# A decoder trunk in float32: the last 512 channels of each sub-layer as one 512-wide piece in halves of K, instead of two pieces of 256

## The chip, the core and the metric

The kernel runs on one core of one Trainium2 chip. The metric is device time in microseconds (us) of one execution; several runs are made and the median is taken. A profiled execution, one more run, gives the trace that is read here. Its times are in us from the start of its span. Engines: PE is TensorE, PEld its weight loads, DVE is VectorE, ACT is ScalarE, POOL is GpSimd, SP is SyncE (its queue issues most DMAs).

## The reference

Two layers over 256 tokens of 2048 channels, in float32. Each layer has two sub-layers, and each sub-layer ends in the same way: a product with a weight matrix, an RMS norm over the 2048 channels of a token, a gain, and the addition to the residual x.

```python
for li in range(DEPTH):                                  # DEPTH = 2
    h = rmsnorm(x, g_mix_pre[li])
    proj = einsum('bsd,de->bse', h, w_in[li])            # 2048 -> 5120
    # four mixers of 512 channels each: gMLP, differential attention, dilated attention, convolution
    mixed = concatenate([out_a, out_b, out_c, out_d], axis=-1)
    x = x + rmsnorm(einsum('bse,ed->bsd', mixed, w_out[li]), g_mix_post[li])
    h = rmsnorm(x, g_ffn_pre[li])
    f = square(relu(einsum('bsd,df->bsf', h, w_ff1[li])))    # 2048 -> 8192
    x = x + rmsnorm(einsum('bsf,fd->bsd', f, w_ff2[li]), g_ffn_post[li])
```

with `rmsnorm(x, g) = x * rsqrt(mean(x*x) + 1e-6) * g`.

## The kernel before

**Numbers in two parts.** Every float32 matrix product is made of three: a value is split into a high part h (rounded to the fp32r type) and a low part l (the rest), and the kernel adds h·h, h·l and l·h. Weights arrive from HBM as "units" of 128 x 1024 floats (512 KB), in the order in which they are used. For each unit ACT makes h (1024 elements per partition) and DVE makes l. `split_hi` and `split_lo` (L251, L261) issue these; a split needs a free buffer pair, of which there are six, and two more from the ending of the mixing on (`room_for`, L269). A buffer is given back by `done(u)` (L289), so a split that reuses it waits for the last matmul of the unit `u`. An h split of ACT in the trace is `h<-w`, an l split of DVE `l<-w,h`.

**Two kinds of products.** In channel form (`unit_c`, `group_c`) the weights are the stationary operand and the tokens stream; the results, tiles `acc` and `accg`, feed the next step. In token form (`unit_t` L432, `units_t` L449, through `mm_t` L406) 128 tokens are stationary and the weights stream; the result has tokens on partitions. `unit_t` makes 512 channels for both halves of the tokens (t = 0, 1) at once: two PSUM tiles `acct`, a unit of 1024 weights covers two steps of K = 128, and for each step kk it calls `mm_t` for t = 0 and t = 1. One `mm_t` is three matmuls.

**A sub-layer's ending** (`sublayer_end`, L681) is what the change touches. There are four of them: mixing and FFN of two layers. Of the 2048 output channels the first three pieces of 512 are made by `unit_t`. The last 512 are made by two calls of `units_t` with n = 256. Each call has four units (a unit covers four steps of K) and makes all of K for the first 128 tokens, tile `accu`, then all of K for the other 128 tokens. So an ending has 4 x 48 = 192 matmuls of 256 columns, and token half 0 is complete 48 matmuls before token half 1. After each accumulation a follow-up is put into the list `soon` (`later`, L378):

- `y_block` (L662) adds the partial sum yt to PSUM (DVE, in FFN endings alone), then squares it with a sum over the channels (ACT, `junk<-accu` or `junk<-yt`, into `sy`), and multiplies by the gain (DVE, `yt<-...,gpb`). For the last piece, n == 4, it returns after the square, and the gain is done beside the Sqrt.
- `last_in` (L695) then, for n == 4, sets the flags calm, held and end, runs `y_rms` (L606: sum, Sqrt on ACT, gain on DVE, reciprocal and two small DVE steps) and puts `turn` into the list `front`, or `finish` in the last ending.
- `turn_part` (L629) handles a quarter of 512 channels of one token half: X is updated on DVE, PE transposes four blocks (`turned`), ACT writes the high part of the next layer's operand (`xhl<-turned,prm`, four steps), and DVE the low part. Then `have[t]` is raised.
- `group_c` (L466) follows at once: the next product. Its blocks are `(0,0), (1,0), (2,0), (0,1), ...` as (quarter, token half); a block (q, 0) has 16 matmuls of 256 columns and needs quarter q of token half 0. So token half 0 is turned while PE still works on token half 1.
- In the last ending `finish` (L654) updates X and writes the output instead.

`sqrt_soon` (L717) runs a tiny Sqrt on ACT between the two calls of `units_t`, so that its table is there.

**What sets the order.** The engines' queues are in program order, and a small planner at build time writes it. `Paced` (L75) keeps a planned clock for each engine, by the cost functions of L117 to L131: a matmul of N columns costs N/2400 + 0.003 us, a DVE step (70 + N)/960 or, for scalar_tensor_tensor, (128 + N)/960, an ACT step (140 + N)/1200. Before every `mm_t` the code calls `pump` (L368), which issues all follow-ups that are due by PE's planned clock. Only there does other work enter the queues. A follow-up is due D_ = 0.13 planned us after what it needs (0.2 for the first step of `later`), and an engine may be ahead of PE's clock by 1.5 planned us at most, 1.0 when the flag end is set. A step (`step`, L357) looks in this order: a split that is needed soon, `soon`, `front`, other splits. With held set, low splits stop. If `group_c` needs a quarter that is not yet issued, `force` (L372) lets time pass without matmuls.

**Buffers.** `pacc` holds four PSUM tiles of one bank; before, a 256-wide `accu` takes one of them.

Of the kernel before, what the change touches and what calls it, by code (L numbers as in the profile page):

```python
# [11 lines left out]
F32 = mybir.dt.float32  # L12
# [3 lines left out]
ALU = mybir.AluOpType  # L16
# [3 lines left out]
P = 128  # L20
L = 2
D = 2048
T = 256
GW = 512
FF = 8192
KD = D // P
# [3 lines left out]
HALF = 8  # L30
# [104 lines left out]
def trunk_kernel(ctx, tc, xT, xt, wu, par, gpost, gw, gb, lam, ndist, mult, out):  # L135
# [9 lines left out]
    tiny = ctx.enter_context(tc.tile_pool(name="tiny", bufs=2))  # L145
    pacc = ctx.enter_context(tc.tile_pool(name="pacc", bufs=4, space=PSUM))
# [8 lines left out]
    V, S = Paced(nc.vector, _dve_cost, PE), Paced(nc.scalar, _act_cost, PE)  # L155
# [121 lines left out]
    def use(u, low=True):  # L277

        state["cur"] = max(state["cur"], u)
        while state["hi"] <= u:  # L280
            split_hi()
        if not low:
            return
        while state["lo"] <= u:
            if state["hi"] <= state["lo"]:
                split_hi()
            split_lo()

    def done(u):  # L289
        wh.pop(u)  # L290
        wl.pop(u)
        pool_of.pop(u)
# [4 lines left out]
    unit = [0]  # L297
    soon, front, queue, lanes, back = [], [], [], [None, None], []
# [32 lines left out]
    def entry(g):  # L331
        return [g, None, lambda: True]
# [35 lines left out]
    def pump():  # L368
        while step():
            pass  # L370

    def force(cond):  # L372
        now = PE.t
        while not cond():
            if not step() and not step(now):
                now += 0.2

    def later(f, n=1):  # L378

        held[0] += n  # L380

        def g():
            yield S, t
            yield from f()
            held[0] -= n

        t = PE.t + 0.2
        soon.append(entry(g()))
# [17 lines left out]
    def mm_t(ps, u, w, xhl, kk, t):  # L406

        h = xhl[:, kk, t * P : (t + 1) * P]
        l = xhl[:, kk, T + t * P : T + (t + 1) * P]
        PE.matmul(ps, h, wh[u][:, w], start=kk == 0, stop=False)  # L410
        PE.matmul(ps, h, wl[u][:, w], start=False, stop=False)
        PE.matmul(ps, l, wh[u][:, w], start=False, stop=kk == KD - 1)
# [33 lines left out]
            done(u)  # L446
        return pss

    def units_t(xhl, n, after):  # L449

        c = HALF * P // n
        units = range(unit[0], unit[0] + KD // c)
        unit[0] += KD // c
        for t in range(2):
            force(lambda: held[0] < 4)
            ps = pacc.tile([P, n], F32, tag="acc", name=f"accu{units[0]}_{t}")
            for kk in range(KD):
                u, k = units[kk // c], kk % c
                use(u)
                pump()  # L460
                mm_t(ps, u, slice(k * n, (k + 1) * n), xhl, kk, t)
                if t == 1 and k == c - 1:
                    done(u)
            later(lambda ps=ps, t=t: after(ps, t))

    def group_c(rhs, have, order, us):  # L466

# [138 lines left out]
    def y_rms(t, sy, beside):  # L606

        yield V, S.t + D_
        ss, a, s, r0, r = [tiny.tile([P, 1], F32, tag=f"y{j}", name=f"y{j}") for j in range(5)]
        V.reduce_sum(ss, sy[:, t, :], axis=AX.X)  # L610
        S.activation(s, ss, AF.Sqrt, bias=epst, scale=1.0 / D)
        V.tensor_scalar(a, ss, -0.5 / D, -0.5 * EPS, ALU.mult, ALU.add)
        beside()
        V.reciprocal(r0, s)
        V.scalar_tensor_tensor(a, a, r0, r0, ALU.mult, ALU.mult)
        V.scalar_tensor_tensor(r, a, 1.5, r0, ALU.add, ALU.mult)
        return r

    def turn(t, r, sx, xhl, li, gcol, have):

        yield None, lambda: True
        if t == 0:
            state["turned"] = 0
        for q in range(4):
            n = TURNS.index((t, q))
            place = sum(e[3] < n for e in front if len(e) > 3)
            front.insert(place, entry(turn_part(t, q, n, r, sx, xhl, li, gcol, have)) + [n])
# [26 lines left out]
    def finish(t, r):  # L654

        yield V, 0.0
        for n in range(4):
            c = slice(GW * n, GW * (n + 1))
            V.scalar_tensor_tensor(X[:, t, c], yt[:, t, c], r, X[:, t, c], ALU.mult, ALU.add)
            Q.dma_start(out[:, t, c], X[:, t, c])  # L660

    def y_block(ps, t, c, n, add, sy):  # L662


        y = yt[:, t, c]
        if add:
            yield V, 0.0
            V.tensor_tensor(y, ps, y, ALU.add)
            ps = y
            yield S, V.t + D_  # L670
        if sy is not None:
            junk = ev.tile([P, GW], F32, tag="junk", name="junk", bufs=1)
            S.activation(junk[:, 0 : c.stop - c.start], ps, AF.Square, accum_out=sy[:, t, n : n + 1])
            if n == 4:
                return ps
            yield V, 0.0
            V.tensor_tensor(y, ps, gpb[:, c], ALU.mult)
        elif not add:
            S.activation(y, ps, AF.Copy)

    def sublayer_end(rhs, first, add, li, gcol, n0=0):  # L681

        nonlocal xhl
        sy = tiny.tile([P, 2, 5], F32, tag="sy", name="sy", bufs=1)
        sx = tiny.tile([P, 2, 4], F32, tag="sx", name="sx", bufs=1)
        have, us = [0, 0], []
        pss = first
        for n in range(3):
            if pss is None:
                pss = unit_t(rhs)  # L690
            for t in range(2):
                later(lambda ps=pss[t], t=t, n=n: y_block(ps, t, slice(GW * n, GW * (n + 1)), n, add, sy))
            pss = None

        def last_in(ps, t, n):  # L695
            c = slice(T * (n + 3), T * (n + 4))
            y = yield from y_block(ps, t, c, n, add, sy)
            if n == 4:
                state["calm"] = state["held"] = state["end"] = li is not None
                r = yield from y_rms(t, sy, lambda: V.tensor_tensor(yt[:, t, c], y, gpb[:, c], ALU.mult))  # L700
                g = finish(t, r) if li is None else turn(t, r, sx, xhl, li, gcol, have)
                front.insert(0, entry(g))

        if li is not None:
            xhl = big.tile([P, KD, 2 * T], F32R, tag="xhl", name="xhl")
        units_t(rhs, T, lambda ps, t: last_in(ps, t, 3))
        sqrt_soon()
        units_t(rhs, T, lambda ps, t: last_in(ps, t, 4))
        if li is None:
            force(idle)  # L710
            return None, None
        state["calm"] = True
        group_c(xhl, have, ((0, 0), (1, 0), (2, 0), (0, 1), (1, 1), (2, 1), (3, None)), us)
        state["calm"] = state["end"] = False
        return us, sx
# [410 lines left out]
def _pack_weights(w_in, w_out, w_ff1, w_ff2):  # L1126

    parts = []

    def blocked(w):  # L1130

        k, n = w.shape
        return w.reshape(k // 1024, 8, P, n // P, P).transpose(3, 0, 2, 1, 4).reshape(n // P, k // 1024, P, 1024)

    def tokens(w):

        n = w.shape[1]
        return w.reshape(-1, 1024 // n, P, n).transpose(0, 2, 1, 3).reshape(-1, P, 1024)

    def grouped(b):  # L1140

        b = b.reshape(2, 2, 2, P, 2, 4 * P)
        return b.transpose(2, 4, 0, 3, 1, 5).reshape(-1, P, 1024)

    def ending(w):
        return [tokens(w[:, n * GW : (n + 1) * GW]) for n in range(3)] + [tokens(w[:, n * T : (n + 1) * T]) for n in (6, 7)]

    for li in range(L):
        w = w_in[li]
        first = []  # L1150
        rest = []
        for kind, grp, i in IN_ORDER:
            if kind == "c":
                b = blocked(w[:, grp * GW + i * P : grp * GW + (i + 1) * P])[0]
            else:
                b = tokens(w[:, grp * GW : (grp + 1) * GW])
            (first if len(first) < 4 else rest).append(b)
        parts.append(grouped(np.stack(first)))
        parts += rest
        wo = np.concatenate([w_out[li][g * GW : (g + 1) * GW] for g in OUT_GROUPS])  # L1160
        parts += ending(wo)
        f1 = blocked(w_ff1[li])
        for blk in range(4):
            b = f1[blk * KD : (blk + 1) * KD]
            if blk == 0:
                parts.append(grouped(b[:4]))
                b = b[4:]
            parts.append(b.reshape(-1, P, 1024))
            b = w_ff2[li][blk * D : (blk + 1) * D]
            parts += ending(b) if blk == 3 else [tokens(b[:, n * GW : (n + 1) * GW]) for n in range(4)]  # L1170
    return np.ascontiguousarray(np.concatenate(parts))
# [48 lines left out]
```

## Time and profile before

| | us |
|---|---|
| median of 3 runs | 2134.38 (2134.36 to 2135.84) |
| profiled execution, its own time | 2133.36 |
| span of the profiled execution | 2131.6 |
| PE busy | 2115.2 |
| PEld busy | 1821.5 |
| DVE busy | 1417.9 |
| ACT busy | 1100.3 |
| mean granted clock of TensorE | 0.998 |

The time of an execution is the span and what lies around it, here 1.8 us. Busy times of engines overlap. An engine's row in the trace gives start and length in us, engine, operation, tile written and tiles read, the shape, and in brackets how long the engine was idle before it and what ended that idle time. Nearly all instructions are issued by a helper, so that their line is L99 everywhere; the tile names tell them apart. The four endings' `accu` pieces begin at 329.2, 1041.0, 1388.7 and 2100.4 us (mixing, FFN, mixing, FFN).

### The profile page before, as it was taken

The page shows a single profiled execution, that of the slowest core. Times are in us where ns is not written, and L with a number is a line of the kernel's source. Part 1 is how long each engine was busy: PE and PEld are TensorE (multiplying, and loading weights), DVE is VectorE, ACT ScalarE, POOL GpSimd, SP SyncE. Part 2 cuts the span into 40 slices and gives each one's busy share as a digit, 9 for nine tenths or more (in the row PEclk, how much of TensorE's full clock was granted, in tenths as well). Part 3 has the DMA queues.
Part 4 walks back from the last instruction along what each step waited for, and adds up shares of the span by engine and source line. Part 5 has one row for each costly group of instructions (what it writes and reads, how often), then busy time and mean ns, then how long its engine had stood idle before and what let it go on. Part 6 is the DMA issues. An engine that isn't in the chain of part 4 may idle for free.

```text
span 2131.6 us, 29947 instructions
## 1 busy us (share of the span) xinstructions
PE 2115.2 (99%) x11404; PEld 1821.5 (85%) x11404; DVE 1417.9 (67%) x2207; ACT 1100.3 (52%) x1711; POOL 9.9 (0%) x57
## 2 busy tenths in 40 slices
PE   9999999999999999999999999999999999999998
PEld 7888889888888888888888888898888888888887
DVE  6889666764665675576579886568547656755754
ACT  6556856554543453454465568565444434434542
POOL 0000000000000000000000000000000000000000
PEclk9999999999999999999999999999999999999999
DMA  7645474565555555555454455646655555555563
GB/s 242 221 147 186 158 237 159 198 226 190 187 197 190 189 192 193 191 192 190 167 171 148 167 170 179 224 159 194 220 196 184 193 197 187 190 197 189 188 197 109
DMA packets 110256, 400.20 MB, mean 188 GB/s; under 512 B 12512, under 2 KB 12800, under 8 KB 109344
## 3 DMA queue, kind: packets, MB, share of 16 engines
q1 hardware_dynamic: 109296, 393.93, 55.2%
q0 software_dynamic: 672, 4.36, 0.6%
q8 instruction: 89, 1.46, 0.3%
q14 instruction: 55, 0.45, 0.1%
q10 hardware_dynamic: 144, 0.01, 0.0%
HBM read 396.15 MB, written 2.10 MB: 187 GB/s over the span
## 4 chain that ended last, share of the span: by engine, by line
PE 96%; DVE 1%; ACT 1%; DMA 1%; issue 0%; DVEq 0%; ACTq 0%
PE acct L99 44%; PE acc L99 42%; PE accu L99 4%; PE accg L99 3%; PE sc L99 1%; DMA w<-in_wu 1%; PE od L99 0%; DVE X L99 0%; PE tr L99 0%; PE turned L99 0%; ACT h L99 0%; PE z L99 0%; DVE l L99 0%; ACT L99 0%; PE ob L99 0%
## 5 line engine op out<-in xcount | busy, mean ns | idle before, releaser
L99 DVE TENSOR_TENSOR l<-w,h 128x1024 fp32r<-128x1024 f32 (+1 forms) x738 | 896.2, 1220 | 543.1 <-ACT h L99 403.9
L99 ACT ACTIVATE h<-w 128x1024 fp32r<-128x1024 f32 (+1 forms) x738 | 775.8, 1055 | 555.0 <-PE acct L99 389.0
L99 PE MATMUL acc<-xhl,h 128*128 128x512 f32 x2560 | 615.6, 391 | 0.0
L99 PE MATMUL acct<-h,f 128*128 128x512 f32 x1920 | 592.4, 389 | 0.0
L99 PEld LDWEIGHTS acc<-xhl,h 128*128 128x128 f32 x2560 | 469.6, 188 | 91.7 <-issue 1.3
L99 PEld LDWEIGHTS acct<-h,f 128*128 128x128 f32 x1920 | 360.4, 188 | 74.7
L99 PE MATMUL acct<-l,f 128*128 128x512 f32 x960 | 373.5, 389 | 0.0
L99 PEld LDWEIGHTS acc<-xhl,l 128*128 128x128 f32 x2560 | 328.6, 191 | 13.2 <-issue 1.0
L99 PE MATMUL acc<-xhl,l 128*128 128x256 f32 x2560 | 335.3, 283 | 0.0
L99 PEld LDWEIGHTS acct<-l,f 128*128 128x128 f32 x960 | 180.2, 188 | 37.1
L99 PE MATMUL acct<-h,xhl 128*128 128x512 f32 x512 | 169.0, 398 | 0.0
L99 ACT ACTIVATE evr<-acc 128x256 f32<-128x256 f32 x160 | 61.4, 385 | 157.3 <-PE acc L99 157.2
L99 ACT ACTIVATE f<-u 128x256 fp32r<-128x256 f32 x120 | 50.1, 417 | 136.7 <-DVE u L99 136.6
L99 PE MATMUL acct<-h,mhl 128*128 128x512 f32 x384 | 120.2, 391 | 0.0
L99 PEld LDWEIGHTS acct<-h,xhl 128*128 128x128 f32 x512 | 96.2, 188 | 20.2 <-issue 0.7
L99 DVE SCALAR_TENSOR_TENSOR cacc<-ch,prm,cacc 128x256 f32<-128x256 f32 x240 | 102.5, 484 | 0.0
L99 PE MATMUL acct<-l,xhl 128*128 128x512 f32 x256 | 100.1, 391 | 1.0 <-DVE l L99 1.0
L99 PE MATMUL accg<-xhl,h 128*128 128x256 f32 (+1 forms) x400 | 89.4, 323 | 6.1 <-DVE xhl L99 6.1
L99 PEld LDWEIGHTS acct<-h,mhl 128*128 128x128 f32 x384 | 72.1, 188 | 14.9
L99 PEld LDWEIGHTS accg<-xhl,h 128*128 128x128 f32 x400 | 65.6, 192 | 11.3 <-DVE xhl L99 4.7
L99 PE MATMUL acct<-l,mhl 128*128 128x512 f32 x192 | 74.7, 389 | 0.0
L99 DVE TENSOR_TENSOR u<-acc,evr 128x256 f32<-128x256 f32 x120 | 50.9, 424 | 23.9 <-ACT evr L99 22.7
(182 smaller groups left out, 1356.1 us busy)
## 6 DMA issues: line engine op xcount, KB each, us to landing
w<-in_wu SPq DMA_DIRECT2D x734, 512.0 KB, 3.3
gpb<-in_gpost POOLq DMA_DIRECT2D x4, 1024.0 KB, 5.1
X<-in_xt SPq DMA_DIRECT2D x2, 1024.0 KB, 6.4
out<-X SPq DMA_DIRECT2D x8, 256.0 KB, 2.0
x_in<-in_xT SPq DMA_DIRECT2D x3, 512.0 KB, 6.5
w<-in_wu SPq DMA_DIRECT2D x4, 256.0 KB, 5.4
wT<-in_gw SPq DMA_DIRECT2D x2, 512.0 KB, 4.4
x_in<-in_xT SPq DMA_DIRECT2D x2, 256.0 KB, 4.6
```

The source lines that it names most:

```text
L99: return f(*a, **k)
```

## The change

A new loop, `units_end`, takes the place of the two calls of `units_t`. It makes the last 512 channels in one piece: two PSUM tiles of 128 x 512, eight units of two steps of K each. It runs the first half of K for token half 0, then for token half 1, then the second half of K for token half 0 and for token half 1: four runs of 24 matmuls of 512 columns. A unit is given back after token half 1 has used it. Token half 0 is complete 24 matmuls before token half 1. The last evacuation of a token half is therefore 512 wide, and there is no separate one of 256 before it; `sy` has four columns instead of five; `sqrt_soon` comes ahead of the whole piece. On the host the weights of the last 512 channels are packed as the other pieces are.

```diff
-    def units_t(xhl, n, after):
...
+    def units_end(xhl, after):
+
+        units = range(unit[0], unit[0] + 8)
+        unit[0] += 8
+        force(lambda: held[0] < 3)
+        pss = [pacc.tile([P, GW], F32, tag="acc", name=f"acce{units[0]}_{t}") for t in range(2)]
+        for half in range(2):
+            for t in range(2):
+                for e in range(4 * half, 4 * half + 4):
+                    use(units[e])
+                    for k in range(2):
+                        pump()
+                        mm_t(pss[t], units[e], slice(k * GW, (k + 1) * GW), xhl, 2 * e + k, t)
+                    if t == 1:
+                        done(units[e])
+                if half == 1:
+                    later(lambda t=t: after(pss[t], t))
...
-            if n == 4:
+            if n == 3:
                 return ps
...
-        def last_in(ps, t, n):
-            c = slice(T * (n + 3), T * (n + 4))
-            y = yield from y_block(ps, t, c, n, add, sy)
-            if n == 4:
...
+        def last_in(ps, t):
+            c = slice(3 * GW, 4 * GW)
+            y = yield from y_block(ps, t, c, 3, add, sy)
...
-        units_t(rhs, T, lambda ps, t: last_in(ps, t, 3))
         sqrt_soon()
-        units_t(rhs, T, lambda ps, t: last_in(ps, t, 4))
+        units_end(rhs, last_in)
...
     def ending(w):
-        return [tokens(w[:, n * GW : (n + 1) * GW]) for n in range(3)] + [tokens(w[:, n * T : (n + 1) * T]) for n in (6, 7)]
+        return [tokens(w[:, n * GW : (n + 1) * GW]) for n in range(4)]
```

More of the change, by code (lines that the diff above doesn't have):

```diff
@@ L447, in unit_t @@
         return pss
-    def units_t(xhl, n, after):
[L451 to L464, printed above, removed]
+    def units_end(xhl, after):
[14 more added lines that the diff above has]
+                    later(lambda t=t: after(pss[t], t))
     def group_c(rhs, have, order, us):
@@ L683, in sublayer_end @@
         nonlocal xhl
-        sy = tiny.tile([P, 2, 5], F32, tag="sy", name="sy", bufs=1)
+        sy = tiny.tile([P, 2, 4], F32, tag="sy", name="sy", bufs=1)
         sx = tiny.tile([P, 2, 4], F32, tag="sx", name="sx", bufs=1)
@@ L693, in sublayer_end @@
             pss = None
-        def last_in(ps, t, n):
-            c = slice(T * (n + 3), T * (n + 4))
-            y = yield from y_block(ps, t, c, n, add, sy)
-            if n == 4:
[L699 to L702, printed above, removed]
+        def last_in(ps, t):
+            c = slice(3 * GW, 4 * GW)
+            y = yield from y_block(ps, t, c, 3, add, sy)
+            state["calm"] = state["held"] = state["end"] = li is not None
+            r = yield from y_rms(t, sy, lambda: V.tensor_tensor(yt[:, t, c], y, gpb[:, c], ALU.mult))
+            g = finish(t, r) if li is None else turn(t, r, sx, xhl, li, gcol, have)
+            front.insert(0, entry(g))
         if li is not None:
             xhl = big.tile([P, KD, 2 * T], F32R, tag="xhl", name="xhl")
-        units_t(rhs, T, lambda ps, t: last_in(ps, t, 3))
         sqrt_soon()
-        units_t(rhs, T, lambda ps, t: last_in(ps, t, 4))
+        units_end(rhs, last_in)
         if li is None:
```

## The prediction

> **What bounds the kernel now.** I read the page's engine line first, then busy time by stretch, then the chain that ended last, then the order of time on each engine around the four sub-layer endings.
>
> ```profile
> PE 2115.2 (99%) x11404; PEld 1821.5 (85%) x11404; DVE 1417.9 (67%) x2207; ACT 1100.3 (52%) x1711; POOL 9.9 (0%) x57
> ```
>
> ```profile
> 1041.00:1098.00 57.00, 56.02 (x431) 53.91 (x430) 40.85 (x88) 35.36 (x85) 0.29 (x4) 1.00 0.40 131
> 1389.00:1445.00 56.00, 54.90 (x430) 53.16 (x429) 39.19 (x82) 35.70 (x85) 0.53 (x1) 1.00 0.45 151
> 2100.50:2131.60 31.10, 23.07 (x193) 22.86 (x191) 13.62 (x31) 5.12 (x16) 0.00 (x0) 0.94 0.18 68
> ```
>
> TensorE is busy 99%, so time can only come from its own pace or from its few gaps. The second fence gives a stretch, its length, then busy us of PE, weight loads, DVE and ACT, the granted clock and the DMA's share. The stretches hold the FFN ending of the first layer, the mixing ending of the second layer, and the tail. PE lacks 1.0 and 1.1 us in the first two, and 8.0 us in the tail. The clock is full there, and the DMA's share of 0.40 to 0.45 speaks against a lack of weights.
>
> ```profile
> 2035.23 65.31 PE acct L99 x288
> 2100.54 23.04 PE accu L99 x192
> ```
>
> These are two pieces of the chain that ended last: start, length, and what ran. Tiles named acct are 512 columns wide, and 65.31/288 is 226.8 ns per matmul. Tiles named accu are the 256-wide pieces that the change replaces, and 23.04/192 is 120.0 ns per matmul. These spacings are the price of a matmul; the means of one in a group include its pipelined end.
>
> **The change part by part.** *Streaming.* Each ending loses 192 matmuls of 256 columns and gains 96 of 512: 23.04 against 96 x 226.8 = 21.77 us. That is 1.27 us less per ending and 5.08 us in four. The new loop alternates between two accumulators in runs of 24; acct alternates after every 3 and holds 226.8, so I take that price. Three quarters of the saving, 0.95 us, comes before the first token half is finished; the other token half then takes 24 x 226.8 = 5.44 us instead of 48 x 120 = 5.76.
>
> Here the page "TensorE: Matmul & The Clock Gate" of the Trainium skill, section "Back-to-back issue gap", gives another price: N/2.4 + 2.5 ns, so 109.2 and 215.8 ns, and an estimate by it is 0.25 us saved per ending. By that price the sum below would end above zero, at about +2.1 us. The rows differ from it, and I go by the rows.
>
> *Evacuation.* Afterwards a token half's last evacuation is 512 wide, where the second 256 were evacuated before.
>
> ```profile
> L99 DVE TENSOR_TENSOR yt<-acct,yt 128x512 f32<-128x512 f32 x44 | 28.7, 682 | 0.0
> ...
> L99 DVE TENSOR_TENSOR yt<-yt,gpb 128x512 f32<-128x512 f32 x12 | 8.3, 692 | 14.1 <-ACT junk L99 14.1
> ...
> L99 ACT ACTIVATE junk<-acct 128x512 f32<-128x512 f32 x12 | 7.2, 599 | 10.1 <-PE acct L99 9.8
> ```
>
> The same steps at 256 columns stand in the rows below at 0.42 (add), 0.41 (gain) and 0.39 us (Square). So the chain from a token half's last matmul to its scale grows by 0.21 for Square, 0.26 for the add (FFN endings alone) and up to 0.28 for the gain, where that is not hidden behind Sqrt. The narrow evacuations that go (two per ending) lay beside matmuls, and their removal is worth nothing.
>
> *Order.* The planner in the code issues other engines' work only at its pump, once per three matmuls. By its cost function a pump now comes every 3 x (512/2400 + 0.003) = 0.649 planned us instead of 0.329. This decides what is queued ahead of Sqrt on ACT.
>
> ```profile
> 1406.08 0.39 ACT L99 ACTIVATE junk<-accu 128x256 f32<-128x256 f32 x1 [3.18 <-PE accu L99]
> 1406.36 0.19 ACT L99 ACTIVATION_READ_ACCUMULATOR junk<-accu 128x1 f32 x1
> 1406.78 0.29 ACT L99 ACTIVATE y<-y,epst 128x1 f32<-128x1 f32 x1 [0.23 <-DVE y L99]
> 1407.46 1.06 ACT L99 ACTIVATE h<-w 128x1024 fp32r<-128x1024 f32 x1 [0.38 <-PE accu L99]
> 1408.90 1.06 ACT L99 ACTIVATE h<-w 128x1024 fp32r<-128x1024 f32 x1 [0.38 <-PE accu L99]
> 1410.06 1.40 ACT L99 ACTIVATE xhl<-turned,prm 128x128 fp32r<-128x128 f32 x5
> 1412.70 0.39 ACT L99 ACTIVATE junk<-accu 128x256 f32<-128x256 f32 x1 [1.24 <-PE accu L99]
> ```
>
> ```profile
> 1406.85 0.41 DVE L99 TENSOR_TENSOR yt<-accu,gpb 128x256 f32<-128x256 f32 x1
> 1407.18 0.15 DVE L99 RECIPROCAL y<-y 128x1 f32<-128x1 f32 x1
> ...
> 1407.82 2.74 DVE L99 SCALAR_TENSOR_TENSOR X<-yt,y,X 128x512 f32<-128x512 f32 x4
> 1411.23 1.13 DVE L99 SCALAR_TENSOR_TENSOR xhl<-turned,prm,xhl 128x128 fp32r<-128x128 f32 x4 [0.67 <-ACT xhl L99]
> ```
>
> ```profile
> 1415.70 1.90 PE L99 MATMUL accg<-xhl,h 128*128 128x256 f32 x14 [0.75 <-DVE xhl L99]
> ```
>
> This is a mixing ending in order of time: start, length, engine, operation. I count from the first token half's Square (1406.08). Before, Square was issued at the pump at 0.329 and planned to end at 0.659, so y_rms came at 0.987, ahead of the first weight split (h), whose buffer is freed at 1.316. Afterwards Square is issued at 0.649, ends at 1.192, and y_rms is due at 1.322: it misses the pump at 1.298 by 0.024. At that pump the split goes out, and Sqrt queues behind it.
>
> The split started at 1.38 and now starts at 1.30 (it waits for a unit of 6 x 226.8 instead of 12 x 120 ns). Sqrt follows 0.96 later (spacing from the FFN rows below), at 2.26 instead of 0.70. The X updates follow another 0.96 later, at 3.22 instead of 1.74: 1.48 later. The transposes slip past a third split. That waits for its unit until 4.02, ends at 5.0, and then xhl's five steps run, at 5.0 instead of 3.98. DVE's part follows after 1.17, at 6.17, and PE's first block 0.40 behind that (FFN rows), at 6.57.
>
> The second token half ends 0.32 earlier, so its Square can start at 6.30 instead of 6.62, when xhl's five steps are done too. PE waits some 0.4 us before the first block. But before, it waited 0.75 us at 1415.70, at the second block, which stands 3.00 us behind the second Square. Now that is 6.30 + 0.21 + 3.00 = 9.51, against 9.62 before. The first block, 16 x 0.12 + 0.36 for transposes, is over at 8.85. So the new wait takes the place of the old one, and each mixing ending gains 0.95 + 0.11 = 1.06 us, 2.1 in two. If nothing of the 1.48 is covered, an ending gives back 0.5; if all is, it gains 1.27.
>
> ```profile
> 1059.20 0.42 ACT L99 ACTIVATE junk<-yt 128x256 f32<-128x256 f32 x1 [3.22 <-DVE yt L99]
> ...
> 1060.12 1.06 ACT L99 ACTIVATE h<-w 128x1024 fp32r<-128x1024 f32 x1 [0.41 <-PE accu L99]
> 1061.08 0.28 ACT L99 ACTIVATE y<-y,epst 128x1 f32<-128x1 f32 x1
> ```
>
> ```profile
> 1058.68 0.42 DVE L99 TENSOR_TENSOR yt<-accu,yt 128x256 f32<-128x256 f32 x1 [1.45 <-PE accu L99]
> ...
> 1062.04 2.74 DVE L99 SCALAR_TENSOR_TENSOR X<-yt,y,X 128x512 f32<-128x512 f32 x4
> 1065.30 0.42 DVE L99 TENSOR_TENSOR yt<-accu,yt 128x256 f32<-128x256 f32 x1 [0.52 <-PE accu L99]
> 1065.64 1.11 DVE L99 SCALAR_TENSOR_TENSOR xhl<-turned,prm,xhl 128x128 fp32r<-128x128 f32 x4
> ```
>
> ```profile
> 1066.04 1.22 PE L99 MATMUL accg<-xhl,h 128*128 128x256 f32 x8 [0.77 <-DVE xhl L99]
> ```
>
> In the FFN ending of the first layer one split already stood ahead of Sqrt. Now the add is planned to end at 1.255 and Square is due at 1.385, after the pump at 1.298. So a split goes ahead of Square (1.36 from 1058.68), Square starts at 2.32 instead of 0.52, and a second split (from 3.0) goes ahead of Sqrt (3.96). X starts at 4.92 instead of 3.36. On DVE two X updates, the second half's add at 6.29, two more X updates and then xhl follow: 8.26 instead of 6.96. PE's first block starts at about 8.66 instead of 7.36. That is 1.3 us, of which 0.95 is paid for by the earlier start: 0.4 us lost. Bounds: 1.27 gained if all is covered, 1.0 lost if the wider gain adds to it and one more split slips in.
>
> ```profile
> 2117.85 0.42 DVE L99 TENSOR_TENSOR yt<-accu,yt 128x256 f32<-128x256 f32 x1 [4.27 <-PE accu L99]
> ...
> 2120.15 2.74 DVE L99 SCALAR_TENSOR_TENSOR X<-yt,y,X 128x512 f32<-128x512 f32 x4
> 2123.61 0.42 DVE L99 TENSOR_TENSOR yt<-accu,yt 128x256 f32<-128x256 f32 x1 [0.72 <-PE accu L99]
> ```
>
> In the tail no weights are left to split, so only widths count: 0.26 + 0.21 + 0.27 = 0.74 per token half. The first half's X starts at 3.04 instead of 2.30 and keeps DVE until 5.7. The 0.72 us that DVE waited are used up, and the second half's add starts at 5.7, as before (5.76). Then its own 0.74 is exposed whole: +0.68 against the 0.95, a gain of 0.27, and at the bounds 0.6 gained or 0.1 lost.
>
> The shorter sum tile (4 columns instead of 5), the earlier preload of Sqrt's table (a step on ACT, which idles half the time, far ahead of the ending's chain) and the weights' new order (same bytes and units, same loads on SP) cost nothing that I can place.
>
> *Sum:* -2.1 (mixing) + 0.4 (FFN) - 0.3 (tail) = -2.0 us. The profiled execution took 2133.36 us (span 2131.6 and 1.8 around it), 1.0 under the median of 2134.38. I forecast the median: 2132.4.
>
> **The rivals.** *The delays are covered.* If the later Sqrt costs nothing in any turn, three endings gain 1.27 and the tail 0.3: -4.1 us, 2130.3. For it: ACT and DVE have idle time in the endings. Against it: PE already waits there for xhl (0.75, 0.77).
>
> *Slower: Sqrt behind the splits decides.* If the first block in a mixing turn comes more than about 1 us after the second token half's end, its delay is no longer covered by the old wait. With the whole 1.48 passed on, each mixing ending loses 0.5 and the FFN ending 1.0, less the tail's 0.3: +1.7 us, 2136.1. For it: the 0.024 us miss, and three splits ahead of xhl. Against it: the cover of 0.75 seen at 1415.70.
>
> *No cheaper matmul.* If 512 columns in halves cost two matmuls of 256 (240 ns), the 5.1 us are gone: +3.1 us, 2137.5. Against it stands acct's row. The price of the Trainium skill's page that is cited above belongs here.
>
> **How the numbers follow.** Chances: forecast 0.65, covered 0.15, Sqrt decides 0.17, no cheaper matmul 0.03. The forecast's own range is 2131.0 to 2133.7. The range reaches into the covered case and to the Sqrt case: 2129.8 to 2135.8. About 0.2% (4.3 us) is what a measurement of this kernel can tell from no change. The whole streaming gain is 5.1 us, so faster by more needs nearly all of it: half of the covered case, 0.08. Slower by more needs 4.3 us of new waits, which only the tails of the last two cases hold: 0.05. The rest, 0.87, is within.
>
> **What would show it.** The chain of waits should show the endings' 96 matmuls in 21.8 us, and the mixing endings' time order an h ahead of the Sqrt, with PE's first block waiting and its second not. In the FFN ending an h should stand ahead of Square and the first block wait 2 us or more; in the tail, the second add should follow X with no gap. The forecast is wrong if a 512 matmul in the endings is not near 227 ns, if Sqrt is not behind a split, or if PE gains gaps away from the endings.

## The result and the profile after

| | us |
|---|---|
| kernel before, median of 4 runs | 2134.37 (2134.17 to 2135.84) |
| changed kernel, median of 4 runs | 2155.02 (2154.70 to 2156.53) |
| ratio | 1.0101, 95% interval 1.0088 to 1.0113 |
| profiled execution of the changed kernel | 2156.53, span 2154.8 |

The change costs 20.6 us, where 2.0 us of gain were forecast. The span of the profiled execution grew by 23.3 us: the profiled execution of the kernel before, 2133.36 us, lies 1.0 under its median, that of the changed kernel 1.5 over. I cut both spans at the matmuls: an ending runs from the first matmul of its last piece to the first one behind `group_c`, a stage from one ending to the next. The last two columns are experiments that are told below.

| us | before | after | five-column sum tile | and earlier y_rms |
|---|---|---|---|---|
| lead-in | 329.38 | 330.04 | 329.56 | 329.94 |
| mixing ending, layer 0 | 50.96 | 57.81 | 57.58 | 50.05 |
| FFN stage, layer 0 | 660.87 | 664.46 | 660.87 | 660.87 |
| FFN ending, layer 0 | 50.88 | 52.24 | 52.12 | 51.88 |
| mixing stage, layer 1 | 296.46 | 296.45 | 296.41 | 296.43 |
| mixing ending, layer 1 | 50.97 | 58.18 | 56.65 | 50.03 |
| FFN stage, layer 1 | 660.87 | 664.46 | 660.87 | 660.87 |
| tail | 31.18 | 31.18 | 30.93 | 30.91 |

So 6.85 + 7.21 = 14.1 us were lost in the two mixing endings, 2 x 3.59 = 7.2 us in the two FFN stages, in which no instruction was changed, and 1.4 us in the FFN ending. The lead-in lies anywhere between 329.0 and 331.5 in kernels that don't touch it, so its 0.7 us says nothing.

The engine line of the page, then two pieces of the chain that ended last, after; then one piece of the kernel before.

```profile
PE 2126.0 (99%) x11020; PEld 1807.3 (84%) x11020; DVE 1416.4 (66%) x2195; ACT 1098.4 (51%) x1695; POOL 9.7 (0%) x57
```

```profile
330.20 21.30 PE acce L99 x93
...
632.29 87.92 PE acct L99 x384
```

```profile
623.85 87.07 PE acct L99 x384
```

PE has 384 matmuls fewer and is still busy 10.8 us longer: 99% again, so this share tells nothing of the loss. The full acct piece in the middle of the FFN stage grew from 226.7 to 229.0 ns per matmul, and the endings' pieces run at 21.30/93 = 229.0 as well.

The mixing ending of the second layer, in order of time on ACT, on DVE and on PE (the first token half's last matmul has just ended):

```profile
1417.68 0.60 ACT L99 ACTIVATE junk<-acce 128x512 f32<-128x512 f32 x1 [2.85 <-PE acce L99]
...
1419.01 1.06 ACT L99 ACTIVATE h<-w 128x1024 fp32r<-128x1024 f32 x1 [0.64 <-PE acce L99]
1419.97 0.28 ACT L99 ACTIVATE y<-y,epst 128x1 f32<-128x1 f32 x1
...
1422.93 0.37 ACT L99 ACTIVATE xhl<-turned,prm 128x128 fp32r<-128x128 f32 x1
1423.69 0.60 ACT L99 ACTIVATE junk<-acce 128x512 f32<-128x512 f32 x1 [0.40 <-PE acce L99]
...
1424.28 1.91 ACT L99 ACTIVATE xhl<-turned,prm 128x128 fp32r<-128x128 f32 x7
```

```profile
1420.93 2.74 DVE L99 SCALAR_TENSOR_TENSOR X<-yt,y,X 128x512 f32<-128x512 f32 x4
1424.41 0.16 DVE L99 TENSOR_REDUCE y<-sy 128x1 f32<-128x4 f32 x1 [0.74 <-ACT junk L99]
...
1427.05 2.74 DVE L99 SCALAR_TENSOR_TENSOR X<-yt,y,X 128x512 f32<-128x512 f32 x4
1429.70 2.15 DVE L99 SCALAR_TENSOR_TENSOR xhl<-turned,prm,xhl 128x128 fp32r<-128x128 f32 x8
```

```profile
1430.20 2.04 PE L99 MATMUL accg<-xhl,h 128*128 128x256 f32 x8 [6.16 <-DVE xhl L99]
```

The h split stands ahead of Sqrt, as forecast. But of the first quarter's four high parts only one is ahead of the second token half's Square on ACT (1423.69). Their low parts come due behind that, and on DVE they stand behind the second half's whole chain: its sum (1424.41), its scale, its four X updates. In the kernel before, the low parts at 1411.23 came right behind the first half's four updates. Here they start at 1429.70, although ACT's first four high parts were ready by about 1425. PE waits 6.16 us for them.

The same ending by stretch: length, busy us of PE, weight loads, DVE, ACT and POOL (with counts), granted clock, DMA share and GB/s.

```profile
1425.00:1430.20 5.20, 0.00 (x1) 0.04 (x1) 4.05 (x10) 2.70 (x10) 0.53 (x1) 0.60 0.58 202
1430.20:1435.00 4.80, 4.80 (x22) 4.80 (x23) 2.35 (x10) 1.14 (x4) 0.00 (x0) 0.50 0.01 3
```

PE does nothing for 5.2 us, and then runs for 4.8 us at half of the clock: eight matmuls of the first block take from 1430.20 to 1432.04, 0.23 us each instead of 0.12. The wait is paid, and then something more.

The FFN ending of the first layer (ACT, DVE, PE) and the tail (DVE):

```profile
1070.45 1.06 ACT L99 ACTIVATE h<-w 128x1024 fp32r<-128x1024 f32 x1 [3.18 <-PE acce L99]
1071.42 0.61 ACT L99 ACTIVATE junk<-yt 128x512 f32<-128x512 f32 x1
```

```profile
1069.10 0.69 DVE L99 TENSOR_TENSOR yt<-acce,yt 128x512 f32<-128x512 f32 x1 [0.56 <-PE acce L99]
...
1073.95 2.74 DVE L99 SCALAR_TENSOR_TENSOR X<-yt,y,X 128x512 f32<-128x512 f32 x4
1076.60 0.68 DVE L99 TENSOR_TENSOR yt<-acce,yt 128x512 f32<-128x512 f32 x1
1077.20 2.15 DVE L99 SCALAR_TENSOR_TENSOR xhl<-turned,prm,xhl 128x128 fp32r<-128x128 f32 x8
```

```profile
1077.60 1.88 PE L99 MATMUL accg<-xhl,h 128*128 128x256 f32 x8 [1.53 <-DVE xhl L99]
```

```profile
2140.42 0.69 DVE L99 TENSOR_TENSOR yt<-acce,yt 128x512 f32<-128x512 f32 x1 [10.91 <-PE acce L99]
...
2143.46 2.74 DVE L99 SCALAR_TENSOR_TENSOR X<-yt,y,X 128x512 f32<-128x512 f32 x4
2146.12 0.68 DVE L99 TENSOR_TENSOR yt<-acce,yt 128x512 f32<-128x512 f32 x1
```

Up to PE's first block both went nearly as the prediction had them: a split ahead of Square, another ahead of Sqrt, the first block 8.50 us behind the first add (forecast 8.66); in the tail X at 3.04 and the second add at 5.70, without a gap. In the FFN ending the second half's add stands behind all four X updates, at 7.50, and not between them at 6.29; the low parts wait for the same work in either order.

What comes behind the first block was not foreseen. The stretches ahead of it and from it on, in the same FFN ending:

```profile
1074.00:1077.60 3.60, 1.81 (x11) 0.91 (x10) 3.60 (x7) 2.39 (x10) 0.00 (x0) 1.00 0.00 0
1077.60:1082.00 4.40, 4.40 (x24) 4.40 (x25) 4.26 (x15) 3.90 (x14) 0.29 (x4) 0.61 0.00 0
```

The clock is halved here too, for 3.4 us from the first block on, although PE's longest wait is 1.53 us.

### The profile page after: what moved, and what is told of

The parts are those of the page before. It is cut to its first block, busy times and chain, and to the rows that moved or that the text cites. A ratio compares the mean times of both kernels' runs of the same rounds, so it can differ in the third digit from the quotient of the medians.

```text
span 2154.8 us, 29134 instructions
## 1 busy us (share of the span) xinstructions
PE 2126.0 (99%) x11020; PEld 1807.3 (84%) x11020; DVE 1416.4 (66%) x2195; ACT 1098.4 (51%) x1695; POOL 9.7 (0%) x57
## 4 chain that ended last, share of the span: by engine, by line
PE 96%; DVE 2%; ACT 1%; DMA 1%; issue 0%; DVEq 0%; ACTq 0%
PE acct L99 43%; PE acc L99 41%; PE accg L99 4%; PE acce L99 4%; PE sc L99 1%; DVE X L99 1%; DMA w<-in_wu 1%; PE od L99 0%; PE turned L99 0%; PE tr L99 0%; ACT h L99 0%; PE z L99 0%; DVE l L99 0%; ACT L99 0%; ACT xhl L99 0%
## 5 line engine op out<-in xcount | busy, mean ns | idle before, releaser
L99 PE MATMUL accg<-xhl,h 128*128 128x256 f32 (+1 forms) x400 | 94.1, 342 | 16.2 <-DVE xhl L99 16.1
L99 PEld LDWEIGHTS accg<-xhl,h 128*128 128x128 f32 x400 | 70.7, 210 | 21.2 <-issue 12.7
```

The lines of the kernel that those rows point to most:

```text
L99: return f(*a, **k)
```

## The experiments

The theory after the result had two parts. **Addresses:** the sum tile of four columns takes 32 bytes where five took 64, so every tile allocated behind it starts 32 bytes lower, and among them are the two extra split buffers, from which PE streams weights from the mixing ending to the end of the layer. **Queue order:** in the mixing endings DVE got the first quarter's low parts behind the second half's chain. The rivals: the FFN stages lose by something else in the change (the packing, the giving back of units); and the mixing endings lose because Sqrt stands behind the split, or because the evacuation is wider, whatever DVE's order.

### Is it the sum tile?

On the changed kernel, five columns are allocated again and four used:

```diff
-        sy = tiny.tile([P, 2, 4], F32, tag="sy", name="sy", bufs=1)
+        sy = tiny.tile([P, 2, 5], F32, tag="sy", name="sy", bufs=1)[:, :, 0:4]
```

> The changed kernel with the tile of channel sums back at five columns (four of them used), so that the tiles allocated behind it start at the same addresses as in the kernel before; in the changed kernel they start 32 bytes lower, and the two extra split buffers of the FFN stages no longer lie on a 64-byte boundary. Theory A (address): in the changed kernel matmuls that stream from these buffers take some 233 ns instead of 226.8, which is the 3.6 us that each FFN stage lost (660.9 to 664.5 us). Here all FFN matmuls are back at 226.8, each FFN stage takes 660.9 us, and the time is 2155.0 - 7.2 - about 0.8 in the endings = 2147.0 us. Theory B (rotation of the accumulators: an ending now takes two PSUM tiles out of the ring of four where it took four): nothing changes, 2155 us.

Measured: 2147.07 us (4 runs), ratio to before 1.0062 (1.0045 to 1.0079). The FFN stages are back at 660.87, the tail gains 0.25 against before, and the mixing endings stay at 57.58 and 56.65. So the tile is all that the FFN stages lost; of the mixing endings' loss it is 0.2 us in the first. The second comes back by 1.5 us, most of which, by the clock readings below, hangs on when the clock falls and not on the tile.

The other way round, on the kernel before alone, an unused tile ahead of all these is grown from 32 to 64 bytes:

```diff
-    tiny.tile([P, 8], F32, tag="even", name="even", bufs=1)
+    tiny.tile([P, 16], F32, tag="even", name="even", bufs=1)
```

> The kernel before with nothing but an unused small tile grown from 8 to 16 columns, which moves all tiles behind it by 32 bytes. Theory A (address): each FFN stage grows from 660.9 to 664.5 us, some matmuls take 233 ns, and the time is 2134.4 + 7.2 + about 0.8 = 2142.4 us. Theory B (rotation of the accumulators): no change, 2134.4 us.

Measured: 2141.0 us (6 runs), ratio 1.0033 (1.0021 to 1.0045); both FFN stages 664.75. No operation differs from the kernel before.

### Which addresses?

I took the condition to be a start at a multiple of 64 bytes, and tried pads of 64, and then of 128, 256 and 512 bytes in the same place (24, 40, 72 and 136 columns), one run of each. The last run leaves the pad alone and puts an unused tile of 32 bytes at the head of the pool of the extra split buffers, so that these alone move.

> The kernel before, its unused tile of 32 bytes grown to 96, so that every tile allocated behind it moves by 64 bytes instead of by 32 (the earlier run with 32 more cost 3.9 us in each FFN stage: 664.75 against 660.87). Nothing is computed otherwise. Theory A (what costs is that the two extra split buffers begin 32 bytes off a multiple of 64): a move by 64 keeps them on it, the FFN stages stay at 660.9 us each and the time at that of the kernel before, some 2133.6. Theory B (any move costs, by the buffers' place against other tiles): FFN stages of 664 to 665 us, time some 2141.

> The kernel before with every tile behind its unused tile moved by 128 bytes. Nothing else is changed. FFN stages stand at 660.87 us without a move, 664.75 with 32 and 664.47 with 64 bytes. Theory A (the extra split buffers must begin at a multiple of 128): 660.9, time some 2133.5. Theory B (a multiple of 256): 664 to 665, time some 2140. Theory C (no alignment, but their distance to what else is accessed at the time): any of the two, and no order with the other pads.

> The kernel before with every tile behind its unused tile moved by 256 bytes. Theories A and B (multiples of 128 or of 256): FFN stages of 660.9 us, time some 2133.5. Theory C (no alignment at this size): 662 to 665, time 2136 to 2141.

> The kernel before with every tile behind its unused tile moved by 512 bytes. Theories A and B: FFN stages of 660.9 us, time some 2133.5. If the pad of 256 costs and this one does not, the multiple is 512; if both cost, no alignment of these sizes is the condition (theory C).

> The kernel before with an unused tile of 32 bytes at the head of the pool of the two extra split buffers, so that these alone move, by 32 bytes. Theory A (their own address costs): FFN stages of 664.7 us as with the 32 bytes ahead of all tiles, time some 2141. Theory B (it is the other tiles that moved with them, residual sums, gains and evacuated tiles, whose accesses collide): 660.9, time some 2133.5.

For seven of the kernels I set the matmuls of the six full acct pieces (384 each) beside the program's, one by one in their order. That tells which buffer each streams from. "Start" is where the extra buffers begin, in bytes past a multiple of 256. The spacings are means in ns.

| kernel | start | one run, us | FFN stage, us | from the extra buffers: h, l | from the six others |
|---|---|---|---|---|---|
| before | 0 | | 660.87 | 226.8, 226.8 | 226.6 to 227.2 |
| after | 224 | | 664.46 | 233.7, 233.4 | 226.7 to 229.8 |
| before, 32 more | 32 | | 664.75 | 234.2, 232.3 | 226.4 to 231.3 |
| before, 64 more | 64 | 2140.03 | 664.47 | 231.4, 228.4 | 226.6 to 232.5 |
| before, 128 more | 128 | 2141.21 | 664.09 | 233.0, 232.1 | 226.6 to 228.0 |
| before, 256 more | 0 | 2132.95 | 660.87 | 226.7, 226.8 | 226.6 to 227.2 |
| before, 512 more | 0 | 2134.87 | 660.87 | | |
| extra buffers alone, 32 more | 32 | 2140.56 | 664.75 | 234.2, 232.5 | 226.5 to 231.2 |

The run with 64 more refuted the 64. What fits all rows is a start at a multiple of 256 bytes: with it the means are at 227, without it those of the matmuls that stream from the moved buffers are above, and in the changed kernel every single one of 552 is slow. Moving these buffers alone gives the whole loss, so the other tiles that moved are not the cause. Some of the six other buffers, which did not move, are slower too in the moved kernels. In every run these six begin at a multiple of 256 bytes, so no run tells a start past such a multiple from an offset against the other buffers. What in the chip collides there stays open.

Three pieces at the same place of the chain, 32 more, 256 more, and the extra buffers alone:

```profile
625.41 88.03 PE acct L99 x384
```

```profile
623.48 87.07 PE acct L99 x384
```

```profile
624.65 88.03 PE acct L99 x384
```

### Does the 0.024 us decide the mixing endings?

On the changed kernel with the five-column tile, y_rms is due 0.03 earlier, so that it meets the pump that it had missed:

```diff
-        yield V, S.t + D_
+        yield V, S.t + D_ - 0.03
```

> The run with five columns of sums, and the step from the sum to the scale due 0.03 planned us earlier, so that it no longer misses the pump at 1.298. That puts the first Sqrt of a mixing ending ahead of the weight split again, and on DVE the low parts of the first quarter ahead of the second token half's sum, scale and X updates. Theory A (queue order costs 7 us in each mixing ending): mixing endings take about 50 us instead of 57.8 and 58.2, and the time is 2147 - 14 = 2133 us. Theory B (the wider evacuation itself, Square 0.60 and gain 0.69 us, makes the ending slow): endings stay above 55 us and the time above 2143 us.

Measured: 2132.63 us (10 runs), ratio 0.9993 (0.9984 to 1.0003). ACT, DVE and PE in the first layer's mixing ending:

```profile
347.43 0.30 ACT L99 ACTIVATE y<-y,epst 128x1 f32<-128x1 f32 x1 [0.22 <-DVE y L99]
347.82 1.06 ACT L99 ACTIVATE h<-w 128x1024 fp32r<-128x1024 f32 x1
```

```profile
352.72 1.13 DVE L99 SCALAR_TENSOR_TENSOR xhl<-turned,prm,xhl 128x128 fp32r<-128x128 f32 x4 [1.24 <-ACT xhl L99]
353.76 0.15 DVE L99 TENSOR_REDUCE y<-sy 128x1 f32<-128x4 f32 x1
```

```profile
353.12 1.94 PE L99 MATMUL accg<-xhl,h 128*128 128x256 f32 x14 [0.36 <-DVE xhl L99]
```

Sqrt is ahead of the split again, the low parts (352.72) are ahead of the second half's sum (353.76), and PE waits 0.36 us. The mixing endings come to 50.05 and 50.03, 0.9 us under before. The evacuation is as wide as in the changed kernel, so its width is not what costs.

### Sqrt behind the split, or DVE's order?

That one due time had set both right. To part them, Sqrt stays behind the split, and only the second half's chain is held until the first quarter's low parts are issued:

```diff
             y = yield from y_block(ps, t, c, 3, add, sy)
+            if li is not None and t == 1:
+                yield None, lambda: have[0] > 0
```

> The run with five columns of sums, with the second token half's sum and scale held back until the first quarter's low parts are issued; Sqrt stays behind the weight split. This parts the two delays. Theory A (DVE's order is what costs: the low parts stood behind the second half's chain and four X updates): mixing endings take about 50 us, time about 2133 us. Theory B (Sqrt behind the split costs by itself, 1.48 us passed on whole): endings take about 51.5 us or more, time 2136 us or more. Theory C (neither, the width): above 2143 us.

```profile
355.38 1.13 DVE L99 SCALAR_TENSOR_TENSOR xhl<-turned,prm,xhl 128x128 fp32r<-128x128 f32 x4 [1.43 <-ACT xhl L99]
356.42 0.15 DVE L99 TENSOR_REDUCE y<-sy 128x1 f32<-128x4 f32 x1
```

```profile
355.79 1.69 PE L99 MATMUL accg<-xhl,h 128*128 128x256 f32 x12 [1.56 <-DVE xhl L99]
```

Measured: 2135.43 us (one run), mixing endings 50.69 and 50.67. Sqrt behind the split alone costs 50.69 - 50.05 = 0.64 us per ending; DVE's order costs 57.58 - 50.69 = 6.9 (6.0 in the second), the halved clock behind the wait included. With Sqrt late and the order kept, an ending is still 0.27 us under before.

The order alone, made on the kernel before, with its pieces of 256 and its early Sqrt: the first half's low parts of a mixing ending are held until the second half's last X update has been issued.

```diff
         if t == 0:
-            state["turned"] = 0
+            state["turned"], state["x1"] = 0, gcol != PG_FFN_PRE
...
+        state["x1"] = state["x1"] or (t, q) == (1, 3)
...
+        if t == 0:
+            yield None, lambda: state["x1"]
```

> The kernel before, its 256-wide pieces and addresses untouched, with DVE's order alone changed in the mixing endings: the low parts of the first token half's quarters are issued behind the second half's sum, scale and four X updates, as in the changed kernel. Theory A (this order is the loss): mixing endings grow from 51.0 to about 57 us, time 2134 + 12 = 2146 us. Theory B (the wide evacuation or the halves of K are needed for the loss): mixing endings stay under 53 us, time under 2138 us.

```profile
354.30:359.90 5.60, 0.27 (x3) 0.07 (x2) 4.21 (x12) 2.84 (x8) 0.53 (x1) 0.93 0.40 155
359.90:364.70 4.80, 4.77 (x22) 4.80 (x23) 2.35 (x10) 1.14 (x4) 0.00 (x0) 0.50 0.09 38
```

Measured: 2149.49 us (one run), mixing endings 58.46 and 57.63. PE waits 5.36 us and then has the same halved clock, without anything else of the change.

### What does the halved clock cost?

24 matmuls of 512 columns, whose results are not read, fill PE's wait. At first I put them at the head of `group_c` (on the kernel with the five-column tile):

> The run with five columns of sums, and 24 matmuls of 512 columns that nobody reads put on PE behind the last product of each mixing ending (into a bank that is free then), so that PE does not idle in the 6 us wait and its clock has no reason to fall. The order of all other work is the same. Theory A (the halved clock after the wait is a cost of its own): the granted clock stays at 1.0 behind the wait, the first 16 matmuls of the next product take 0.12 us each instead of 0.25, mixing endings fall from 57.6 and 56.7 to about 55 us, time 2142 us. Theory B (DVE and ACT set the pace behind the wait, the clock is hidden): mixing endings stay at 57 us, time 2147 us.

```profile
351.74 5.62 PE L477 MATMUL accg<-mhl 128*128 128x512 f32 x24
357.20 0.60 PE L99 MATMUL turned<-ident,X 128*128 128x128 f32 x4
362.98 2.04 PE L99 MATMUL accg<-xhl,h 128*128 128x256 f32 x8 [5.19 <-DVE xhl L99]
```

Measured: 2156.79 us, mixing endings 62.20 and 62.39. There they stood ahead of the second quarter's transposes (357.20), and held up the chain itself: PE then waited 5.19 us all the same, and the clock fell. That run says nothing about the clock. Moved behind the transposes, right ahead of the first block:

```diff
+            for _ in range(24 if busy is not None and (q, t) == (0, 0) else 0):
+                nc.tensor.matmul(sc[:, 1, :], busy[:, 0, 0:P], busy[:, 0, :], start=True, stop=True)
```

> The changed kernel with the four-column sum tile, and in each mixing ending 24 unread 512-wide matmuls right ahead of group_c's first block, behind the transposes of the second quarter, so that the chain on ACT and DVE is not held. They take 24 x 0.227 = 5.4 us of a wait of some 6 us; their results are not read and nothing else is left out. Theory A (the idle stretch costs twice: by itself, and by the halved clock that is granted after it): the clock stays at 1.0 through the first blocks, these matmuls take 0.12 us each and not 0.25, and the mixing endings come to about 55 us in place of 57.6 and 56.7, the time to some 2142. Theory B (the halved clock is paid anyway, or PE is not what bounds the stretch after the wait): endings of 56.5 to 57.6 as without the matmuls, time about 2147.

As built, the sum tile has five columns here too, of which four are used, so the run compares with 2147.07.

The stretches from the last transposes on, of the kernel without them and then with them:

```profile
352.30:358.50 6.20, 0.07 (x1) 0.00 (x0) 4.56 (x12) 3.74 (x14) 0.53 (x1) 0.86 0.47 169
358.50:363.60 5.10, 5.06 (x24) 5.09 (x25) 2.65 (x11) 1.14 (x4) 0.00 (x0) 0.50 0.00 0
```

```profile
352.80:358.50 5.70, 5.70 (x27) 4.43 (x25) 3.87 (x10) 3.94 (x14) 0.54 (x1) 1.00 0.46 171
359.20:364.00 4.80, 4.77 (x40) 4.80 (x41) 3.36 (x14) 2.85 (x10) 0.00 (x0) 1.00 0.01 3
```

Measured: 2143.44 us (one run, 3.6 under 2147.07), endings 55.28 and 55.27. With the clock at 1.00, PE starts 40 matmuls and transposes in 4.8 us instead of 24 in 5.1. PE's first block begins 28.98 us into the first ending in both. The halved clock costs 57.58 - 55.28 = 2.3 us of the first ending, and 1.4 of the second; the rest is the wait. The two differ by when the clock falls: without the unread matmuls it is 0.50 for 6.8 us in both endings, but in the first this begins 1.8 us before the first block and leaves 5.1 us of work at half the clock, in the second 3.8 us before, which leaves 3.0. In the changed kernel's second ending it left 6.1, and that ending took 58.18.

### The same order in the FFN ending

The FFN ending still lost 1.0 us against before. On the version with the earlier y_rms, Square of the FFN's last piece is made due 0.1 earlier, so that it comes ahead of the split:

```diff
-            yield S, V.t + D_
+            yield S, V.t + D_ - (0.1 if n == 3 and sy is not None else 0.0)
```

> The run with the earlier due time, and in the last piece of an FFN ending Square due 0.1 planned us earlier, so that it goes ahead of the weight split again. The planner then, though, puts the second token half's sum and scale ahead of the first quarter's low parts on DVE in the FFN ending. Theory A (DVE's order decides, not the place of Square and Sqrt): the FFN ending grows from 51.9 to 55 us or more, time 2136 us or more. Theory B (the splits ahead of Square and Sqrt are the FFN ending's loss): it falls to about 51 us, time 2131.7 us. Mixing endings stay at 50.0 in both.

```profile
1064.26 0.16 DVE L99 TENSOR_REDUCE y<-sy 128x1 f32<-128x4 f32 x1
...
1069.03 2.16 DVE L99 SCALAR_TENSOR_TENSOR xhl<-turned,prm,xhl 128x128 fp32r<-128x128 f32 x8
```

Measured: 2136.64 us (one run), FFN ending 56.83. X starts 1.5 us earlier behind its add than in the changed kernel (3.33 us behind 1056.85, against 4.85), and yet PE waits 6.39 us: the low parts (1069.03) now slipped behind the second half's chain here too.

I then tried a finer grain on the same version, a pump ahead of each matmul of the last piece instead of each third:

> Both due times earlier, five columns of sums, and the planner's pump called before each matmul of the last piece instead of once in three, 0.216 planned us apart. On paper this gives the order of the kernel before in mixing endings and puts Square ahead of the split and the low parts ahead of the second half's add in the FFN ending. Theory A (only order and address stood against the wide piece): mixing endings 50.0 us or less, FFN ending 50.0 us or less (50.9 before), tail 30.9, time 1.0 + 1.9 = about 3 us under the kernel before. Theory B (the wide evacuation costs the FFN ending its gain in any order): FFN ending 51.5 us or more, time 1 us under the kernel before.

Measured: 2145.58 us (5 runs), ratio 1.0057 (1.0043 to 1.0071); mixing endings 53.67 and 53.65, FFN ending 55.95. Neither theory had this. PE in the mixing ending:

```profile
360.32 1.98 PE L99 MATMUL accg<-xhl,h 128*128 128x256 f32 x8 [3.73 <-DVE xhl L99]
```

The first quarter's low parts are now in time, and the second quarter's stand behind the second half's four updates. PE waits 3.73 us, one block later.

Last, both due times with the hold of the second half's chain, which fixes the order instead of leaving it to the plan:

> The version with two earlier due times (0.03 before the sum of squares in the mixing endings, 0.1 before the first X updates in the FFN endings), the four-column sum tile, and the second half's accumulator chain held until the first quarter's low parts have been issued. Theory A (the endings lose only by DVE's queue order: whoever keeps the first quarter's low parts ahead of the second half's chain and updates keeps PE fed): mixing endings 50.0 us as with the one earlier due time, FFN ending 50.9 to 51.4 (before 50.9, with the one earlier due time 51.9), tail 30.9; together 1.3 to 2.5 us under the kernel before, 2131.2 to 2132.4. Theory B (the FFN ending is bound by the second half's add, which waits for PE between the X updates and keeps the low parts behind it in either order): FFN ending 51.9 or more, the time that of the one earlier due time, 2132.6, or above it.

Here too the sum tile is built with five columns, of which four are used, and what is due 0.1 earlier in the FFN endings is Square.

```profile
1062.21 1.41 DVE L99 SCALAR_TENSOR_TENSOR X<-yt,y,X 128x512 f32<-128x512 f32 x2
1064.33 0.69 DVE L99 TENSOR_TENSOR yt<-acce,yt 128x512 f32<-128x512 f32 x1 [0.70 <-PE acce L99]
1064.93 1.41 DVE L99 SCALAR_TENSOR_TENSOR X<-yt,y,X 128x512 f32<-128x512 f32 x2
1066.55 1.13 DVE L99 SCALAR_TENSOR_TENSOR xhl<-turned,prm,xhl 128x128 fp32r<-128x128 f32 x4 [0.21 <-ACT xhl L99]
1067.59 0.15 DVE L99 TENSOR_REDUCE y<-sy 128x1 f32<-128x4 f32 x1
```

Measured: 2131.51 us (11 runs) against 2133.61 of the kernel before (15 runs), ratio 0.9991 (0.9982 to 1.0000). Mixing endings 50.05 and 50.05, FFN ending 50.91, tail 30.91. By stages that is -0.91 - 0.92 + 0.03 - 0.27 = -2.1 us against before, and the medians differ by 2.1. It is the fastest version of this case, and its gain is at the edge of what can be measured.

## Why the prediction was wrong, point by point

By the terms of the sum, in us: mixing endings -2.1 forecast, +14.1 measured; FFN ending +0.4 and +1.4; tail -0.3 and 0.0; and the FFN stages, which the sum did not hold, +7.2.

- **Streaming** was right with the buffers where they had been: 512 columns cost 226.8 ns in the halves too (21.09 us for 93 matmuls with the five-column tile; 229.0 in the changed kernel). The rival "no cheaper matmul" falls. The estimate of 215.8 ns from the Trainium skill's page "TensorE: Matmul & The Clock Gate", section "Back-to-back issue gap", falls with it.
- **"The shorter sum tile (4 columns instead of 5) ... cost nothing that I can place"** failed: 7.2 us in the FFN stages. I counted instructions and bytes, and not where the tiles behind it would stand.
- **Order on ACT** was right up to the X updates. From the first Square, Sqrt was forecast at 2.26 and X at 3.22; in the trace they are at 1419.97 - 1417.68 = 2.29 and 3.25. The miss by 0.024 us was real, and undoing it by 0.03 brings 0.91 and 0.94 per mixing ending, where 1.27 was forecast if nothing of the delay were left. But of xhl's five steps, forecast ahead of the second Square at 6.30, one stands ahead of it, and that Square is at 1423.69 - 1417.68 = 6.01.
- **"DVE's part follows after 1.17, at 6.17"** is the step that lost the most. It lies at 1429.70 - 1417.68 = 12.02, and PE's first block at 12.52 instead of 6.57. I took over the duration from the kernel before, and with it the order: that nothing would stand between the high parts and the low parts. I had asked what goes ahead of Sqrt on ACT, and did not ask what the second half's chain, due 0.32 us earlier, goes ahead of on DVE. The "old wait covers the new one" fell with it; and even where the order is held, the cover is in part: Sqrt behind the split leaves 0.27 us of gain per ending, not 1.06.
- **The rival "Sqrt behind the splits decides"** had the right wait, that of the first block, and neither its cause nor its price. Alone the late Sqrt costs 0.64 us per mixing ending (1.7 us in all were forecast, FFN and tail included); DVE's order costs 6 to 7.
- **FFN ending:** right up to the first block, and short of what follows. X started at 4.85 instead of 4.92 and the low parts at 8.10 instead of 8.26. Counted from the ending's first matmul, the first block lies at 25.29 us in the changed kernel and 25.02 with clean addresses, against 24.83 before: +0.46 and +0.19, where 0.35 was forecast. Yet the ending lost 1.36 in the changed kernel, 1.24 with clean addresses and 1.0 with the earlier y_rms too. The sum put nothing behind the first block: in the first two, 3.4 us at half the clock cost up to 1.7; in the third the clock stays at 1.00, and the third block waits 1.03 us instead of 0.20. The 0.95 of earlier start is there: in the last run the first add comes 16.52 us into the ending instead of 17.47. But PE's waits in it are 2.13 us instead of 0.97, which takes back nearly all of the 1.27 that streaming saves: 50.91 against 50.88.
- **Tail:** -0.27 forecast, -0.25 and -0.27 measured with clean addresses; in the changed kernel the slower streaming took it back (31.18).

## What to carry to other kernels

Where a planner writes the queues, a change of grain moves every due time: follow the order on each engine that feeds PE, not only on the engine where the first miss is seen, and ask which of two independent chains comes first on it. Two chains that are ready at nearly the same time, of which one feeds PE, should be ordered by a condition and not by a plan's estimate. A tile that shrinks moves all tiles behind it: compare the addresses of buffers that PE streams from, and check a stage that the change does not touch.

## What the runs showed of the hardware

With all split buffers at a multiple of 256 bytes, matmuls that stream 512 columns of fp32r come every 226.8 ns. With the extra ones 32, 64, 128 or 224 bytes past one, matmuls that stream from these come every 231 to 234 ns (h parts), some 3% more, and some that stream from the unmoved ones slow down as well, up to 232.5. The Trainium skill's page "SBUF — State Buffer", section "Operand start alignment", asks only for a multiple of the element size and says that it speaks of legality, not of speed. All starts here meet that rule, and the runs add a price in time.

After PE's waits of 3.7 to 6.4 us the granted clock was 0.50 for another 2.9 to 6.1 us of work, and the same stretch filled with unread matmuls kept it at 1.00; in the kernel before, after a wait of 0.75 us, it stayed at 1.00. The half-rate stretches of the mixing and FFN endings last 3.4, 6.8 or 10.2 us, part of them still in the wait. The length of one wait does not settle it: with 1.53 us in the FFN ending the clock fell in the changed kernel, and with the earlier y_rms, after the same wait, it did not. The Trainium skill's page "TensorE: Matmul & The Clock Gate", section "What's actually happening", has the array fall to half its clock after an idle window of some 3.4 us and come back after as long a busy one. The rows of the long waits fit the fall; for the return they show up to 6.1 us of work at half the clock. So a wait of 6 us cost up to 8.5.
